# Token-tile stores and loads moved from SP's queue to ACT's, and eighteen expert-weight chunks allowed ahead of the gathers

## The chip, the cores and the metric

The kernel runs on one core of one Trainium2 chip. The metric is the device time of one execution in microseconds (us), and the number quoted for a kernel is the median of several executions.

## The reference

Two layers of a diffusion trunk work on 512 latent tokens and 256 context tokens of width 1024. Each layer normalises its rows, mixes the tokens in four head groups (HGRN2, Hyena, neighbourhood attention, latent attention), adds the result through one output projection, and then adds a mixture of 32 expert MLPs in which every token goes to its top two experts. Cut to the part around the change:

```
x  = x + g1 * (concat(o_a, o_b, o_c, o_d) @ w_out[l])           # residual rows
h2 = rmsnorm(x, norm2_g[l]) * (1 + s2) + sh2                    # normalised rows
lg = h2 @ wg + bg ; le = h2 @ we + be                           # router: 4 groups, 8 experts in each
wts = softmax(top_2(le of the best group)) * p(best group)
y   = sum over the 2 experts e of  wts * ((silu(h2 @ w_gate[e]) * (h2 @ w_up[e])) @ w_down[e])
x  = x + g2 * y                                                 # layer 0 does this for the context rows too
```

Layer 0 handles 768 tokens, which are six tiles of 128; layer 1 handles only the 512 latent tokens, four tiles.

## The kernel before, in words

After the mixers of a layer, the output projection is done in four column blocks `c` (the matmuls have line L1787). In the last block, each finished tile of 128 tokens is passed, two tiles later (`LAG = 2`), to `token_tile(t)`. That function stores the residual rows to DRAM (L1753, into `acc` in layer 0 and into the output in layer 1), transposes the rows on TensorE (L1757), takes the row's inverse root mean square (`row_rs`, whose square on ACT is L1170), copies the transposed rows out of PSUM on ACT (L1759), and multiplies them by the router's weights (L1762). Every fourth tile it also loads the norm gain (`E.load`, L170) and the two modulation rows (`bc_row`, L1511), and VectorE joins two of them (L1766). VectorE then scales the rows (L1768), GpSimd adds the shift (L1769), the normalised rows are stored to DRAM (L1770, `h2d`), and VectorE finishes the logits (L1772). The router (`rt.tile`, VectorE rows L891 to L936 with ACT rows L905 and L912) follows tile by tile, one tile behind, and `rt.finish()` builds the tables from which the gathers know which token goes where.

The MoE then works through the experts in blocks of 64 tokens. GpSimd gathers the normalised rows of a block (128 half rows of 2 KB) from `h2d` with an indirect DMA (L990), TensorE transposes them (L1000), multiplies by the gate and up weights (L1012) and by the down weights (L1039), and GpSimd scatters the weighted result into the residual (L1052).

The expert weights are 201 MB in each layer: 32 experts of six chunks of 1 MB. `Weights.fetch` issues one DMA for each chunk (L1378) on SP's queue into one of 18 slots, so three experts fit. A slot is loaded again when the matmuls that read it are done. Among the chunks that are fetched without an `after`, chunk q also waits until chunk q - 5 has landed (`FLIGHT = 5`). `EARLY` sets how many chunks are fetched before the token tiles (4 in layer 0, 7 in layer 1), and `FIRST` up to which chunk SP goes on without waiting for the first gather: 12 in layer 0 and 16 in layer 1. The rest of the first 18 chunks waits in `moe` for the first gather, by `wts.fetch(18, E.gathered)` at L1109. Ten of the slots lie in a buffer named `side`, which the mixers use before, and the others in `arena`.

Each engine's queue runs its instructions, DMA issues among them, in order: an issue that waits holds back everything behind it on that engine. A scheduler lays out the instructions of each engine ahead of time, so the program order of one engine can change wherever an instruction changes its engine. The completion of a DMA is signalled by one of a few semaphores, which all the queues fed by SP and ACT share; a DMA that takes up such a semaphore again waits until the DMA that used it before has landed.

Of the kernel before, what the change touches and what calls it, by code (L numbers as in the profile page):

```python
# [18 lines left out]
P = 128  # L19
NLAT, NCTX, NTOK = 512, 256, 768  # L20
DM = 1024
# [93 lines left out]
class Env:  # L115
# [48 lines left out]
    def p2(self):  # L164
        return self._ps("pa", 1024, 2)

    def load(self, tag, ap, bufs=1):

        t = self.t(tag, list(ap.shape[1:]), bufs=bufs, rows=ap.shape[0])
        self.nc.sync.dma_start(t, ap)  # L170
        return t

    def const(self, name, ap, dt=F32):
# [991 lines left out]
def row_rs(E, x, tag):  # L1165

    nc = E.nc
    rs = E.t(tag, 1, bufs=2)
    junk = E.t(tag + "j", DM, BF16, bufs=1)
    nc.scalar.activation(junk, x, AF.Square, accum_out=rs)  # L1170
    nc.vector.tensor_scalar(rs, rs, 1.0 / DM, EPS, op0=ALU.mult, op1=ALU.add)
    small_rsqrt(E, rs, tag)
    return rs
# [176 lines left out]
STEPS1 = [1] * 2  # L1350
STEPH1 = 13
HLM = 2
FIRST = (12, 16)
FLIGHT = 5
LAG = 2
AHEAD = 1
# [41 lines left out]
def half_rows(a, t):  # L1398

    return a[t * 256:(t + 1) * 256].rearrange("(p a) c -> p (a c)", a=2)  # L1400


def trunk(tc, d, out):
    nc = tc.nc
# [6 lines left out]
    with ExitStack() as top:  # L1411
# [3 lines left out]
        E = Env(tc, Arena(), None, cst)  # L1415
# [19 lines left out]
        h2d = [dr.tile([2 * (NTOK, NLAT)[l], 512], F32, name=f"h2d{l}") for l in range(2)]  # L1435
        acc = [dr.tile([2 * NTOK, 512], F32, name="acc"), out.rearrange("t (a c) -> (t a) c", a=2)]
# [65 lines left out]
        for l in range(2):  # L1502
# [2 lines left out]
            both = PARTS if full else PARTS[:1]  # L1505
            NQ = nt * P

            def bc_row(v, i, tag, bufs):
                r = E.t(tag, DM, bufs=bufs)
                a = modd[l][v:v + 1, i * DM:(i + 1) * DM]  # L1510
                nc.sync.dma_start(r, bass.AP(tensor=a.tensor, offset=a.offset, ap=[[0, P], [1, DM]]))  # L1511
                return r

            if l:
# [167 lines left out]
            def wo_half(c, h, load, cut):  # L1682

                if not h and load:
                    wos[c] = [wpools[c % 2][1].tile([P, 8, 256], F32R, tag=g, name=f"{g}{l}{c}", bufs=1) for g in ("woh", "wol")]
                hs = slice(h * 128, h * 128 + 128)
                if load:
                    raws[c, h] = wsc.t("wo", [8, 128], F32, 2, P)
                    nc.sync.dma_start(raws[c, h], d[f"w_out{l}"][c][:, :, hs])
                if cut:  # L1690
                    split_r(E, *(w[:, :, hs] for w in wos[c]), raws[c, h], 1)
# [25 lines left out]
            x1 = [E.t("x1", DM, bufs=nt) for _ in range(nt)]  # L1717
# [4 lines left out]
            br = E.load("br", d[f"b_rt{l}"])  # L1722
            n2c = E.load("n2c", d[f"n2c{l}"])
            g1 = [bc_row(v, 2, "g1", 2) for v in range(2 if full else 1)]


# [23 lines left out]

            def token_tile(t):
                v = t // 4
                nc.sync.dma_start(half_rows(acc[l], t), x1[t])  # L1753
                hTt = E.t("h2T", [8, P], bufs=1)
                pt = E.p2()
                for j in range(8):
                    nc.tensor.transpose(pt[:, j * P:(j + 1) * P], x1[t][:, j * P:(j + 1) * P], E.c["ident"])  # L1757
                rs = row_rs(E, x1[t], "rs2")
                nc.scalar.copy(hTt, pt.rearrange("p (j t) -> p j t", j=8))  # L1759
                ps = E.p1()  # L1760
                for j in range(8):
                    nc.tensor.matmul(ps[:, :36], hTt[:, j], wa[v][:, j], start=(j == 0), stop=(j == 7))  # L1762
                if t % 4 == 0:
                    n2 = E.load("h2", d[f"n2g{l}"], bufs=2)
                    mod[:] = [bc_row(v, 4, "rsc", 1), bc_row(v, 3, "rsh", 1)]
                    nc.vector.scalar_tensor_tensor(mod[0], mod[0], 1.0, n2, op0=ALU.add, op1=ALU.mult)  # L1766
                h2 = E.t("h2", DM, bufs=2)
                nc.vector.scalar_tensor_tensor(h2, x1[t], rs, mod[0], op0=ALU.mult, op1=ALU.mult)  # L1768
                nc.gpsimd.tensor_add(h2, h2, mod[1])  # L1769
                nc.sync.dma_start(half_rows(h2d[l], t), h2)  # L1770
                lg = E.t("rlg", 36, bufs=2)
                nc.vector.scalar_tensor_tensor(lg, ps[:, :36], rs, cb[v], op0=ALU.mult, op1=ALU.add)  # L1772
                return lg

            mod, logits = [], []
            for c in range(4):
                if c:
                    wo(c)
                woh, wol = wos[c]
                for t in range(nt + LAG * (c == 3)):  # L1780
                    if t < nt:
                        tt, cc = slice(t * P, (t + 1) * P), slice(c * 256, c * 256 + 256)
                        ps = E.pw()
                        i = 0
                        for o_, w in ((oh, woh), (oh, wol), (ol, woh)):
                            for k in range(8):
                                nc.tensor.matmul(ps[:, :256], o_[:, k, tt], w[:, k, :], start=(i == 0), stop=(i == 23))  # L1787
                                i += 1
                        tmp = E.t("xo", 256, bufs=2)
                        nc.vector.tensor_mul(tmp, ps[:, :256], g1[t // 4][:, cc])  # L1790
                        nc.gpsimd.tensor_add(x1[t][:, cc], x1[t][:, cc], tmp)  # L1791
                    if c == 3 and t >= LAG:
                        logits.append(token_tile(t - LAG))
                        if t > LAG:
                            rt.tile(t - LAG - 1, logits[t - LAG - 1])
# [9 lines left out]
            wts.grow(18 - len(wts.slots))  # L1805
            wts.fetch(FIRST[l])
            sps.close()
# [4 lines left out]
            for v in range(2 if full else 1):  # L1812
                g = E.t("g2", 512, bufs=2)
                a = modd[l][v:v + 1, 5 * DM:]
# [134 lines left out]
```

## Time and profile before

| what | value |
|---|---|
| median of 3 runs | 2420.07 us (2411.84 to 2425.87) |
| the profiled execution | 2419.79 us |
| its span, first to last instruction | 2418.0 us |
| mean granted TensorE clock | 0.956 of full speed |
| busy shares of the span | PE 84%, DVE 41%, ACT 24%, POOL 22% |

The profiled execution took 2419.79 us, 1.8 us more than its span and 0.3 us less than the median of the runs, so it stands for them well. Below, PE is TensorE's matmuls, DVE is VectorE, POOL is GpSimd, SP is the sync engine whose work here is to issue DMAs, and "SPq" is its queue. Times in the views count from the start of the span. In layer 0 the token tiles run from about 745 to 805 us and the MoE from 818 us to about 1320 us; in layer 1 the token tiles run from about 1865 to 1900 us and the MoE from 1916 us to the end.

### The profile page before, as it was taken

Reading aid. Unit: us, or ns where it says so; the run is one execution under the profiler, and the core shown is the slowest. Engines: PE = TensorE matmul, PEld = TensorE weight load, DVE = VectorE, ACT = ScalarE, POOL = GpSimd, SP = SyncE. Lnnn points to the kernel's source line nnn. Section 1 sums busy time; section 2 is a strip of 40 time slices with the busy share of each in tenths; the row PEclk is TensorE's granted clock in tenths of the full one; section 3 lists DMA queues with packets and bytes.
Section 4 is the critical chain, followed back from the end, with each engine's and each line's share of the span. In section 5 each row is a group of like instructions: output and inputs, shape, how many; then the busy total and the mean of one; then the engine's idle time right before and its main releaser. Section 6 shows DMA issues by size and latency. Waiting matters only on the chain. (4 is left out here: it accounts for less than half of the span.)

```text
span 2418.0 us, 32200 instructions
## 1 busy us (share of the span) xinstructions
PE 2039.0 (84%) x11540; PEld 1186.2 (49%) x11540; DVE 999.4 (41%) x2435; ACT 573.2 (24%) x1138; POOL 537.2 (22%) x429
## 2 busy tenths in 40 slices
PE   5789999999999598887777598999899598877775
PEld 1458778766688333322222386686669333222221
DVE  6751865537746522221112437645584511111110
ACT  4433431344622100000000234314352100000000
POOL 1653413211013122211111225131102221111111
PEclk9999999999998699999999799999999699999998
DMA  6434524202244899999999425420233899999996
GB/s 242 165 116 176 194 105 147 81 9 69 85 143 142 299 378 387 405 401 404 400 395 411 173 92 175 147 103 18 86 126 133 313 393 410 409 408 409 410 403 258
DMA packets 139311, 581.54 MB, mean 241 GB/s; under 512 B 23984, under 2 KB 47873, under 8 KB 88630
## 3 DMA queue, kind: packets, MB, share of 16 engines
q1 hardware_dynamic: 124054, 555.89, 59.5%
q0 software_dynamic: 15008, 22.36, 3.9%
q8 instruction: 152, 2.49, 0.4%
q14 instruction: 97, 0.79, 0.1%
HBM read 554.17 MB, written 36.80 MB: 244 GB/s over the span
## 5 line engine op out<-in xcount | busy, mean ns | idle before, releaser
L1012 PE MATMUL pb<-side,arena 128*64 128x512 f32 x1224 | 288.9, 604 | 45.9 <-DMA side<-in_w_moe 42.2
L1016 DVE COPY arena<-pb 128x512 f32<-128x512 f32 x67 | 46.3, 691 | 501.5 <-PE pb L1012 501.5
L1012 PE MATMUL pb<-arena 128*64 128x512 f32 x920 | 217.9, 605 | 41.8 <-DMA arena<-in_w_moe 38.2
L1028 ACT ACTIVATE arena<-pb 128x256 f32<-128x256 f32 x67 | 25.7, 383 | 902.9 <-PE pb L1025 902.9
L1276 POOL TENSOR_TENSOR wl<-side,wh 128x1024 fp32r<-128x1024 f32 x52 | 125.4, 2412 | 395.5 <-ACT wh L1275 267.1
L1012 PEld LDWEIGHTS pb<-side,arena 128*64 128x64 f32 x1224 | 81.4, 137 | 246.5 <-issue 126.4
L1300 PE MATMUL pw<-hh,wh 128*128 128x512 f32 (+1 forms) x720 | 168.6, 366 | 3.1 <-DVE arena L495 1.9
L1300 PE MATMUL pw<-hh,wl 128*128 128x512 f32 (+1 forms) x720 | 160.5, 358 | 0.0
L1043 DVE SCALAR_TENSOR_TENSOR arena<-pb,arena 128x512 f32<-128x512 f32 x67 | 50.3, 750 | 263.2 <-PE pb L1039 254.5
L1039 PE MATMUL pb<-side,arena 128*64 128x512 f32 x576 | 137.8, 617 | 24.9 <-DVE arena L1029 20.4
L1300 PE MATMUL pw<-hl,wh 128*128 128x512 f32 (+1 forms) x720 | 158.2, 355 | 0.0
L1012 PEld LDWEIGHTS pb<-arena 128*64 128x64 f32 x920 | 62.2, 138 | 190.8 <-issue 96.0
L1052 POOL DMA_INDIRECT acc<-arena x35 | 55.2, 1577 | 387.8 <-DVE arena L1047 338.5
L1300 PEld LDWEIGHTS pw<-hh,wh 128*128 128x128 f32 x720 | 117.8, 190 | 36.1 <-issue 14.4
L1039 PE MATMUL pb<-arena 128*64 128x512 f32 x496 | 115.5, 599 | 21.3 <-DVE arena L1029 20.8
L1300 PEld LDWEIGHTS pw<-hh,wl 128*128 128x128 f32 x720 | 117.9, 189 | 25.1 <-issue 9.9
L1300 PEld LDWEIGHTS pw<-hl,wh 128*128 128x128 f32 x720 | 117.4, 189 | 24.4 <-issue 8.7
L1052 POOL DMA_INDIRECT out_dram<-arena x32 | 50.9, 1590 | 311.4 <-DVE arena L1043 297.2
L990 POOL DMA_INDIRECT arena<-h2d,arena x67 | 69.8, 1042 | 187.5 <-issue 56.0
L1791 POOL TENSOR_TENSOR arena<-arena 128x256 f32<-128x256 f32 x40 | 31.2, 782 | 292.2 <-DVE arena L1790 278.2
L1025 PE MATMUL pb<-ident,arena 128*128 128x128 f32 x268 | 42.4, 280 | 55.4 <-DVE arena L1016 55.4
L1039 PEld LDWEIGHTS pb<-side,arena 128*64 128x64 f32 x576 | 39.0, 140 | 101.5 <-issue 60.8
(367 smaller groups left out, 3444.2 us busy)
## 6 DMA issues: line engine op xcount, KB each, us to landing
side<-in_w_moe SPq DMA_DIRECT2D x215, 1024.0 KB
arena<-in_w_moe SPq DMA_DIRECT2D x169, 1024.0 KB
arena<-in_w_ada SPq DMA_DIRECT2D x53, 512.0 KB
side<-in_w_in SPq DMA_DIRECT2D x52, 512.0 KB
side<-in_w_ada SPq DMA_DIRECT2D x43, 512.0 KB
arena<-in_w_out SPq DMA_DIRECT2D x16, 512.0 KB
arena<-in_x SPq DMA_DIRECT2D x12, 512.0 KB
spd<-arena SPq DMA_DIRECT2D x23, 256.0 KB
```

What stands on the lines that cost most here:

```text
L990: E.gathered = nc.gpsimd.indirect_dma_start(out=xg, out_offset=None, in_=h2d, in_offset=bass.IndirectOffsetOnAxis(ap=gi, axis=0), **(dict( ...
L1012: nc.tensor.matmul(pg[64 * s:64 * s + 64], xT[:, j // 4, j % 4, :], W[j // 2][:, (j % 2) * 1024 + s * 512:(j % 2) * 1024 + s * 512 + 512], ...
L1016: nc.vector.tensor_copy(gu, pg)
L1025: nc.tensor.transpose(pt[:, c * 128:(c + 1) * 128], gu[:, c * 128:(c + 1) * 128], E.c["ident"])
L1028: nc.scalar.activation(hT, pv[:, :, 0, :], AF.Silu)
L1039: nc.tensor.matmul(pd[64 * s:64 * s + 64], hT[:, c, :], W[4 + c // 2][:, (c % 2) * 1024 + s * 512:(c % 2) * 1024 + s * 512 + 512], start=( ...
L1043: nc.vector.scalar_tensor_tensor(y, pd, w[0], g2[0], op0=ALU.mult, op1=ALU.mult)
L1052: E.nc.gpsimd.indirect_dma_start(out=acc, out_offset=bass.IndirectOffsetOnAxis(ap=si, axis=0), in_=y, in_offset=None, compute_op=ALU.add, ...
L1276: (nc.vector if k % 2 else nc.gpsimd).tensor_sub(lo, src, hi.bitcast(F32))
L1300: nc.tensor.matmul(ps[:, :n], w[:, j, :], h[:, j, a:a + n], start=(i == 0), stop=(i == 23))
L1791: nc.gpsimd.tensor_add(x1[t][:, cc], x1[t][:, cc], tmp)
```

## The change

Three things are edited. The two stores of `token_tile` (L1753, L1770) are issued from ACT's queue instead of SP's. The loads of the norm gain and of the two modulation rows in `token_tile` go to ACT's queue as well, through a new argument `queue` of `load` and `bc_row`. That is 18 DMAs in layer 0 (6 + 6 stores, 2 gain loads, 4 modulation rows) and 11 in layer 1 (4 + 4, 1, 2). And `FIRST` becomes 18 in both layers, so chunks 12 to 17 of layer 0 and 16 and 17 of layer 1 no longer wait for the first gather.

```
-    def load(self, tag, ap, bufs=1):
+    def load(self, tag, ap, bufs=1, queue=None):
         t = self.t(tag, list(ap.shape[1:]), bufs=bufs, rows=ap.shape[0])
-        self.nc.sync.dma_start(t, ap)
+        (queue or self.nc.sync).dma_start(t, ap)
...
-FIRST = (12, 16)
+FIRST = (18, 18)
...
-            def bc_row(v, i, tag, bufs):
+            def bc_row(v, i, tag, bufs, queue=nc.sync):
                 r = E.t(tag, DM, bufs=bufs)
                 a = modd[l][v:v + 1, i * DM:(i + 1) * DM]
-                nc.sync.dma_start(r, bass.AP(tensor=a.tensor, offset=a.offset, ap=[[0, P], [1, DM]]))
+                queue.dma_start(r, bass.AP(tensor=a.tensor, offset=a.offset, ap=[[0, P], [1, DM]]))
...
             def token_tile(t):
-                nc.sync.dma_start(half_rows(acc[l], t), x1[t])
+                nc.scalar.dma_start(half_rows(acc[l], t), x1[t])
...
-                    n2 = E.load("h2", d[f"n2g{l}"], bufs=2)
-                    mod[:] = [bc_row(v, 4, "rsc", 1), bc_row(v, 3, "rsh", 1)]
+                    n2 = E.load("h2", d[f"n2g{l}"], bufs=2, queue=nc.scalar)
+                    mod[:] = [bc_row(v, 4, "rsc", 1, nc.scalar), bc_row(v, 3, "rsh", 1, nc.scalar)]
...
-                nc.sync.dma_start(half_rows(h2d[l], t), h2)
+                nc.scalar.dma_start(half_rows(h2d[l], t), h2)
```

What stands on SP's queue in layer 0 from the fourth token tile on, before (the expert chunks are L1378 and the rows L1815 load the output gate of the MoE):

```order
L170 DMA arena<-in_n2g 128x1024
L1378 DMA side_6263<-in_w_moe 128x2048
L1770 DMA h2d_70<-arena 128x1024
L1511 DMA arena<-modd_66 128x1024 x2
L1753 DMA acc<-arena 128x1024
L1378 DMA side_6263<-in_w_moe 128x2048
L1770 DMA h2d_70<-arena 128x1024
L1378 DMA side_6263<-in_w_moe 128x2048
L1770 DMA h2d_70<-arena 128x1024
L1378 DMA side_6263<-in_w_moe 128x2048 x5
L1815 DMA arena<-modd_66 128x1x512 x2
```

The first three chunks stand between stores and loads of the token tiles, and the other five behind the last store. SP's queue at the same place after the change, from the last loads of the output projection's weights (L1689) on:

```order
L1719 DMA arena<-in_x 128x1024 x3
L1689 DMA arena<-in_w_out 128x8x128 x4
L1378 DMA side_6263<-in_w_moe 128x2048 x10
L1378 DMA arena<-in_w_moe 128x2048 x4
L1815 DMA arena<-modd_66 128x1x512 x2
```

No store and no token-tile load is left between the chunks, and the four `arena` chunks (14 to 17) stand ahead of the gate loads and of the first gather.

ACT's queue in the middle of layer 0's token tiles, around the loads of the second set of gain and modulation rows (L905 and L912 are router rows):

```order
+L1770 DMA h2d_70<-arena 128x1024
 L905 ACTIVATE arena<-arena 128x4
-L1759 COPY arena<-pa_5849 128x1024
+L1759 COPY arena<-pa_6030 128x1024
+L170 DMA arena<-in_n2g 128x1024
+L912 ACTIVATE arena<-arena 128x1
+L1511 DMA arena<-modd_66 128x1024 x2
+L905 ACTIVATE arena<-arena 128x4
+L912 ACTIVATE arena<-arena 128x1
+L1753 DMA acc<-arena 128x1024
```

The loads of the second set now stand behind the copy L1759 of the fifth tile (`pa_6030`).

ACT's queue in the token tiles of layer 1, from the first tile's copy on:

```order
 L1759 COPY arena<-pa_19343 128x1024
+L1770 DMA h2d_71<-arena 128x1024
+L1753 DMA out_dram<-arena 128x1024
+L1770 DMA h2d_71<-arena 128x1024
+L1759 COPY arena<-pa_19408 128x1024
+L905 ACTIVATE arena<-arena 128x4
+L912 ACTIVATE arena<-arena 128x1
 L1170 ACTIVATE arena<-arena 128x1024
-L905 ACTIVATE arena<-arena 128x4
-L1759 COPY arena<-pa_19408 128x1024
-L912 ACTIVATE arena<-arena 128x1
+L1753 DMA out_dram<-arena 128x1024
```

The square L1170 of the third tile, which stood ahead of the second tile's copy, now stands behind two stores of normalised rows, that copy and two router rows. Layer 0 has the same pattern at its third tile.

## Rows read from the trace of the kernel before

**Rows 1.** Waits on SP's queue, 942:1320 (total us, times, longest):
```profile
SPq L1378 <- DMA side<-in_w_moe: 169.8, 71, 3.5
```

**Rows 2.** Windows: busy per engine, then PEclk, DMA share, GB/s:
```profile
770.00:830.00 60.00, 36.09 (x181) 25.09 (x179) 38.82 (x242) 9.82 (x24) 13.85 (x10) 0.60 0.81 277
905.00:930.00 25.00, 22.58 (x112) 8.20 (x110) 6.24 (x10) 1.94 (x4) 4.21 (x3) 1.00 0.94 355
1935.00:1940.00 5.00, 5.00 (x26) 1.65 (x24) 0.75 (x1) 0.00 (x0) 1.63 (x1) 1.00 0.80 292
2220.00:2240.00 20.00, 14.03 (x68) 4.85 (x68) 2.98 (x5) 1.94 (x4) 2.63 (x2) 1.00 1.02 410
```

**Rows 3.** SP's timeline, 1025 to 1085 us (start, length, count):
```profile
1032.65 19.74 SPq L1378 DMA_DIRECT2D arena<-in_w_moe  x8
1083.22 0.33 SPq L1378 DMA_DIRECT2D arena<-in_w_moe  x1
```

**Rows 4.** Waits on SP's queue, 770 to 835 us:
```profile
SPq L1770 <- POOL arena L1769: 22.4, 3, 14.4
```

**Rows 5.** SP's timeline, 745 to 830 us:
```profile
776.56 1.21 SPq L1511 DMA_DIRECT2D arena<-modd  x2
778.33 0.44 SPq L1378 DMA_DIRECT2D side<-in_w_moe  x1
793.62 0.42 SPq L1378 DMA_DIRECT2D side<-in_w_moe  x1
820.57 1.42 SPq L1378 DMA_DIRECT2D side<-in_w_moe  x2
```

**Rows 6.** Waits on SP's queue, 905 to 942 us:
```profile
SPq L1378 <- PE pb L1012: 12.7, 9, 4.3
SPq L1378 <- PE pb L1039: 10.4, 4, 5.4
```

**Rows 7.** SP's timeline, three stretches between 905 and 926 us:
```profile
905.29 0.33 SPq L1378 DMA_DIRECT2D side<-in_w_moe  x1
912.64 5.48 SPq L1378 DMA_DIRECT2D side<-in_w_moe  x4
925.00 0.33 SPq L1378 DMA_DIRECT2D side<-in_w_moe  x1
```

**Rows 8.** ACT's timeline, token tiles of layer 0, then layer 1:
```profile
782.76 1.01 ACT L1759 COPY arena<-pa 128x1024 f32<-128x1024 f32 x1 [0.23 <-PE pa L1757]
1874.60 1.06 ACT L1170 ACTIVATE arena<-arena 128x1024 bf16<-128x1024 f32 x1 [4.91 <-DVE arena L1772]
1879.83 0.29 ACT L912 ACTIVATE arena<-arena 128x1 f32<-128x1 f32 x1 [1.74 <-DVE arena L891]
```

**Rows 9.** VectorE's timeline, 786 to 792 us:
```profile
787.73 1.22 DVE L1766 SCALAR_TENSOR_TENSOR arena<-arena 128x1024 f32<-128x1024 f32 x1
791.10 2.13 DVE L892 SCALAR_TENSOR_TENSOR arena<-arena,miota 128x4 f32<-128x4 f32 x1
```

**Rows 10.** GpSimd's timeline, layer 0 and layer 1:
```profile
812.19 1.25 POOL L990 DMA_INDIRECT arena<-h2d,arena  x1 [13.30 <-DVE arena L948]
1874.34 2.35 POOL L1769 TENSOR_TENSOR arena<-arena 128x1024 f32<-128x1024 f32 x1 [2.11 <-DVE arena L1768]
1882.41 2.37 POOL L1769 TENSOR_TENSOR arena<-arena 128x1024 f32<-128x1024 f32 x1 [3.11 <-DVE arena L1768]
1911.46 1.07 POOL L990 DMA_INDIRECT arena<-h2d,arena  x1 [18.84 <-DVE arena L964]
```

**Rows 11.** TensorE's timeline, 817 to 820 us:
```profile
818.01 1.09 PE L1000 MATMUL pb<-ident,arena 128*128 128x128 f32 x4 [8.17 <-DMA arena<-h2d,arena]
```

**Rows 12.** Waits on SP's queue, 1876 to 1920 us:
```profile
SPq L1770 <- POOL arena L1769: 15.3, 3, 6.1
```

**Rows 13.** Waits and timeline of SP's queue, 1920 to 1955 us:
```profile
SPq L1378 <- PE pb L1012: 11.0, 6, 5.3
1935.50 0.82 SPq L1378 DMA_DIRECT2D arena<-in_w_moe  x2
```

## The prediction, made before the changed kernel ran

> **What bounds the kernel now.** I read the waits of SP's queue first, since the change is about that queue. In the long stretch of layer 0's MoE, 942 to 1320 us, SP stands in front of expert chunks until earlier chunks have landed: 169.8 us for the `side` slots alone [rows 1]. The reader should then look at the busy windows: in the MoE of layer 1 the DMA engines are full (share 1.02 at 410 GB/s) while TensorE is busy for 14.03 of 20 us [rows 2]. So the MoE is bound by moving weights, and the pace can be read off: 18 chunks lie between the issues at 1032.65 and 1083.22 (eight issues from the first row on, ten in `side` slots, then the second row) [rows 3], which is 50.57 / 18 = 2.81 us per chunk, 16.9 us per expert of six. A microsecond in which the engines stand idle before the end of that stream costs a microsecond, unless something else sets the stream's place.
>
> The token tiles are the place where they idle. From 770 to 830 us the DMA share is 0.81 [rows 2], so 60 x 0.19 = 11.4 us of the engines' time is free there, and SP stands 22.4 us in front of stores of normalised rows, waiting for GpSimd's addition [rows 4]. The chunk behind the issue at 778.33 goes out only at 793.62, 15.3 us later [rows 5]; and the last six of layer 0's first 18 chunks wait for the gather and go out from 820.57 [rows 5]. In layer 1 the same wait is 15.3 us [rows 12].
>
> But a lead gained here must survive the start of the MoE. There are only 18 slots, and a slot comes free when TensorE has read it. From 905 to 942 us SP waits 12.7 + 10.4 = 23.1 us for TensorE's matmuls [rows 6], and in layer 1 11.0 us between 1920 and 1955 [rows 13]. There the stream is placed by TensorE, which started when the gathers landed. Chunks that were fetched earlier only make SP reach full slots earlier.
>
> **Part 1: the lead, layer 0.** Six chunks may go out before the gather, worth 6 x 2.81 = 16.9 us if nothing else limited them. What can be kept is the work that the engines still have in hand at the last slot that TensorE gives late. At 905.29 a chunk is issued [rows 7] and, by the limit of five in flight, at most 5 x 2.81 = 14.1 us of chunks are outstanding, done at 919.4. Four more issues begin at 912.64 [rows 7], 11.2 us more, done at 930.6. The next, which TensorE sets, comes at 925.00 [rows 7]. So at that moment 5.6 us of chunks are in hand; with a longer lead they would have landed before, and the chunk of 925.00 would land up to 5.6 us sooner. Bounds: 5.6 and 0 (the share of 0.94 from 905 to 930 [rows 2] says that the engines idled for 1.5 us even so). I take 4, since the backlog was worked out with five in flight at 905.29, the most there can be.
>
> **Part 2: the lead, layer 1.** Two chunks, 5.6 us at most, and 0 at least. The four chunks that TensorE released before 1935.50 are nearly through by then: the share falls to 0.80 in 1935 to 1940 [rows 2], just where the next pair is issued [rows 13]. I take 2.
>
> **Part 3: ACT waits in order.** One issue takes SP 0.33 us [rows 7]; if it takes ACT as long, the 29 DMAs are 9.6 us in two layers. In the token tiles of layer 0 ACT was busy for 9.82 of 60 us [rows 2], and the issues lie in its idle time, so I cost the issuing at nothing; without that cover it would be the 9.6 us. What counts are the waits behind which ACT's other rows now stand.
>
> In layer 1, the square of the third tile began at 1874.60 [rows 8]. Now it stands behind the store of the second tile's normalised rows, which waits for the addition of 1874.34 + 2.35 = 1876.7 [rows 10], and behind a copy and two router rows, the last of which ended at 1879.83 + 0.29 = 1880.1 [rows 8]. It can start at 1880.1 at the earliest, 5.5 us later. Its result is wanted by VectorE's scaling, whose addition on GpSimd began at 1882.41 [rows 10], so some of the 5.5 us is covered. If the tiles slide, GpSimd's additions fall among more of VectorE's last router rows, and beside an addition a VectorE row of some 0.2 us took 2.13 us [rows 9]. Bounds for the gather of layer 1: 0 and 7 us (5.5 and most of one such row); I take 3.
>
> In layer 0 the same pattern stands at the third tile, and the second set of modulation rows adds to it. Their loads were issued at 776.56 [rows 5]; on ACT they stand behind the copy that ended at 782.76 + 1.01 = 783.8 [rows 8], so they go out at least 7.2 us later. VectorE's row that joins them ran at 787.73 without an idle gap ahead of it [rows 9], 11.2 us after the issue; VectorE runs in order, so the router's rows wait behind it when it is late. If the loads land as slowly as 11.2 us, and the chunks now share the engines with them, the row moves to 783.8 + 11.2 = 795.0, 7.3 us later. If they land in under 3.9 us, it does not move. VectorE has router rows pulled ahead of it in the new order that fill some of the gap. Bounds for the gather of layer 0: 0 and 8; I take 2.
>
> **Part 4: gathers beside chunks.** The first gather of layer 0 began at 812.19 and TensorE used it at 818.01 [rows 10, 11], 5.8 us. Until now no chunk was issued between; now chunks 14 to 17 may be. Four chunks in full would be 4 x 2.81 = 11.2 us, but the gather moves 128 half rows of 2 KB, a quarter of a chunk, and goes from GpSimd's own queue. If the engines take turns, it needs its own 2.81 / 4 = 0.7 us once more. Bounds 0 and 3, I take 1 in each layer.
>
> A rule speaks against the whole change. The Trainium skill, "DMA: Bandwidth & Descriptors", section "Issuing engines are not separate DMA queues", says that DMAs from different engines end on the same 16 DMA engines and interleave, and that a second issuing engine saves only the sequencer's time to issue. By that rule alone the change would be worth the 9.6 us of issuing, none of it on the path. The trace disagrees in one point: SP's 22.4 us is a wait in order for a semaphore, not issuing, and that wait does leave the chunks' queue.
>
> **Part 5: the attention.** The scheduler has also moved the first set of loads (L1511) into ACT's stream amid the softmax. Nothing waits for them there for a long time; I take 0, with 2 us either way.
>
> **The sum.** Layer 0: 2 + 1 - 4 = -1. Layer 1: 3 + 1 - 2 = +2. Together +1 on the profiled 2419.79, or on the median of 2420.07, which lies 0.3 us off: 2421. With every term at its good end: -5.6 - 5.6 - 2 = -13, 2407. At its bad end: 8 + 7 + 3 + 3 + 2 = +23, 2443.
>
> **The rivals.** *The lead counts in full.* If slots were not the limit, eight chunks of 2.81 us, 22.5 us, would be kept: 2397. For it: the engines' free 11.4 us before the gather. Against it: SP's 23.1 us and 11.0 us of waits for TensorE. Chance 0.16.
>
> *Slower: the first gather of both layers is late.* TensorE's start sets the place of the stream, so a late gather is paid in full while the lead is lost in the slots. With 8 + 7 from ACT's order and 3 + 3 from the sharing: 2441. It decides from about 6 us in each layer, which makes 12 us, half a per cent. For it: an ACT row 5.5 us late in layer 1 and loads 7.2 us late in layer 0. Against it: the addition at 1882.41 leaves the third tile some cover, and the loads have slack where they land in less than 11.2 us. Chance 0.19.
>
> *The change does not do what it says.* The queues of SP and ACT share the semaphores on which completions are counted, so chunks 5 to 13 still wait until certain of ACT's stores and loads have landed, and chunk 14 takes its slot from a tile that the router frees only at its end. Then the lead is one or two chunks, and it is lost as above: 2420. Chance 0.12.
>
> **How the numbers follow.** The forecast holds 0.53, with its own range 2411 to 2432. Half a per cent, 12 us, is about what a measurement of this kernel tells from no change. Faster by more than that: the first rival and a little of the forecast, 0.19. Slower: the second rival and the forecast's far end, 0.21. Within: 0.60. The range leaves out the first rival alone, and takes in the second: 2402 to 2442.
>
> **What would show it.** Right: no store left on SP's queue, chunks 4 to 13 issued one behind the other from 772 us, the first gathers 1 to 5 us later than 812.19 and 1911.46, longer waits of SP for TensorE in the first experts, and the same 2.81 us per chunk afterwards. Wrong to the fast side: the last late slot of layer 0 at 920 or sooner, or no wait for TensorE at all. Wrong to the slow side: gathers more than 6 us late, or TensorE's first matmul more than 6 us behind its gather.

## The result, and the profile after

The changed kernel took 2430.07 us in the median of 12 runs (2425.72 to 2440.34), the kernel before 2416.29 us in the median of 12 runs on the same chips. The ratio is 1.0064 with a 95% interval of 1.0051 to 1.0076, so the change costs 15 us, 12 to 18. The time lies inside the range of 2402 to 2442, but it is not the forecast of 2421: it is slower by a little over half a per cent, which had a chance of 0.21.

The profiled execution of the changed kernel has a span of 2425.8 us, 7.8 us more than before. That difference has to be taken apart, because a part of it lies where nothing was changed. I cut both spans at the same landmarks: the first matmul of the output projection (L1787), the issue of the first gather (L990), the first transpose of gathered rows (L1000), and the last up matmul of the layer (L1012). Here is TensorE's timeline of the kernel before at these landmarks (start, length):

```profile
684.40 1.19 PE L1787 MATMUL pw<-woh,oh 128*128 128x256 f32 x8
...
833.40 7.09 PE L1012 MATMUL pb<-arena 128*64 128x512 f32 x32 [2.04 <-ACT arena L1002]
...
1332.16 1.94 PE L1012 MATMUL pb<-side,arena 128*64 128x512 f32 x8 [0.67 <-DMA side<-in_w_moe]
...
1820.12 0.50 PE L1787 MATMUL pw<-woh,oh 128*128 128x256 f32 x2
...
1916.62 1.12 PE L1000 MATMUL pb<-ident,arena 128*128 128x128 f32 x4 [7.45 <-DMA arena<-h2d,arena]
...
2394.80 1.94 PE L1012 MATMUL pb<-side,arena 128*64 128x512 f32 x8 [0.96 <-SPq L1129]
```

The same of the changed kernel:

```profile
679.74 1.20 PE L1787 MATMUL pw<-woh,oh 128*128 128x256 f32 x8
...
821.76 1.09 PE L1000 MATMUL pb<-ident,arena 128*128 128x128 f32 x4 [10.00 <-DMA arena<-h2d,arena]
...
837.75 8.78 PE L1012 MATMUL pb<-arena 128*64 128x512 f32 x32 [2.67 <-ACT arena L1002]
...
1337.86 1.94 PE L1012 MATMUL pb<-side,arena 128*64 128x512 f32 x8 [0.57 <-DMA side<-in_w_moe]
...
1824.70 0.50 PE L1787 MATMUL pw<-woh,oh 128*128 128x256 f32 x2
...
1924.36 1.11 PE L1000 MATMUL pb<-ident,arena 128*128 128x128 f32 x4 [10.73 <-DMA arena<-h2d,arena]
...
2402.56 1.94 PE L1012 MATMUL pb<-side,arena 128*64 128x512 f32 x8 [0.28 <-SPq L1129]
```

GpSimd's timeline of the changed kernel, the first gather of each layer, which answers to [rows 10]:

```profile
814.12 1.25 POOL L990 DMA_INDIRECT arena<-h2d,arena  x1 [10.97 <-DVE arena L948]
...
1915.92 1.03 POOL L990 DMA_INDIRECT arena<-h2d,arena  x1 [11.37 <-DVE arena L964]
```

The differences of these rows give the stretches:

| stretch (us) | before | after | difference |
|---|---|---|---|
| layer 0: projection starts, to first gather issued | 127.79 | 134.38 | +6.6 |
| layer 0: first gather issued, to first transpose | 5.82 | 7.64 | +1.8 |
| layer 0: first transpose, to end of last up matmul | 516.09 | 518.04 | +2.0 |
| layer 1: projection starts, to first gather issued | 91.34 | 91.22 | -0.1 |
| layer 1: first gather issued, to first transpose | 5.16 | 8.44 | +3.3 |
| layer 1: first transpose, to end of last up matmul | 480.12 | 480.14 | 0.0 |

The six together are +13.6 us, which agrees with the medians. The rest of the span is 5.8 us shorter: layer 0's projection starts at 679.74 instead of 684.40, in front of which only the first set of modulation rows and the order of a few rows beside it have changed, and 1.1 us is gained between the MoE of layer 0 and the projection of layer 1. Over the ten kernels of this study that start lies anywhere between 678.2 and 687.5 us without a pattern, so it is the spread of single executions, and the stretches are what I compare below.

**Where the lead went.** SP's timeline of the changed kernel, layer 0:

```profile
764.83 29.65 SPq L1378 DMA_DIRECT2D side<-in_w_moe  x10
811.17 2.01 SPq L1378 DMA_DIRECT2D arena<-in_w_moe  x4
```

The queue did what the diff says: no store stands between the chunks, the ten `side` chunks leave between 764.83 and 794.5 us, and the next four at 811.17, ahead of the gather. The six chunks that waited until 820.57 [rows 5] are all early. SP is not free of ACT's DMAs, though. A chunk that takes up a semaphore again waits for the store or load that used it last, so these waits stand in front of the chunks from 740 to 830 us, 25.3 us together:

```profile
SPq L1378 <- DMA h2d<-arena: 14.1, 2, 11.3
SPq L1378 <- DMA arena<-modd: 5.8, 2, 3.6
SPq L1378 <- DMA arena<-in_n2g: 5.4, 1, 5.4
```

Now look at the busy windows of the changed kernel (columns as in [rows 2]), right after the gathers and around the place where the prediction put the last late slot:

```profile
825.00:840.00 15.00, 12.11 (x51) 4.40 (x49) 1.11 (x2) 2.73 (x4) 1.44 (x2) 0.84 0.26 86
900.00:950.00 50.00, 45.27 (x222) 16.52 (x220) 13.50 (x22) 3.88 (x8) 8.46 (x6) 1.00 0.91 341
```

and of the kernel before:

```profile
825.00:840.00 15.00, 12.75 (x66) 5.32 (x64) 1.11 (x2) 2.73 (x4) 1.01 (x1) 1.00 1.02 365
900.00:950.00 50.00, 44.59 (x218) 16.29 (x216) 12.66 (x20) 3.87 (x8) 9.48 (x7) 1.00 0.98 380
```

From 825 to 840 us the DMA engines are busy for 0.26 of the time, where they were full before: all 18 slots are taken and none is free. TensorE goes through the first expert's weights twice, since its tokens fill two blocks, and the second block reads the same `arena` slots from 837.75 us on (the rows at 833.40 and 837.75 above); SP's next chunk leaves at 840.28. That is 11 us of idle engines, and the second window adds (0.98 - 0.91) x 50 = 3.5 us. Most of the 16.9 us of the lead is given back there. SP's waits from 830 to 960 us show it from the other side, 70 us for TensorE where the same rows of before come to 23.8 us (13.4 and 10.4):

```profile
SPq L1378 <- PE pb L1012: 50.8, 21, 16.6
SPq L1378 <- PE pb L1039: 19.5, 8, 6.5
```

**Where the time was lost.** ACT's timeline of the changed kernel (ACTq are the issues on its queue):

```profile
755.64 1.01 ACT L1759 COPY arena<-pa 128x1024 f32<-128x1024 f32 x1 [7.47 <-POOL arena L1769]
774.34 0.33 ACTq L1770 DMA_DIRECT2D h2d<-arena  x1
776.38 0.30 ACT L905 ACTIVATE arena<-arena 128x4 f32<-128x4 f32 x1 [5.17 <-DVE arena L904]
778.75 0.81 ACTq L1511 DMA_DIRECT2D arena<-modd  x2
...
1882.66 1.01 ACT L1759 COPY arena<-pa 128x1024 f32<-128x1024 f32 x1 [7.39 <-POOL arena L1769]
```

and VectorE's:

```profile
791.03 1.22 DVE L1766 SCALAR_TENSOR_TENSOR arena<-arena 128x1024 f32<-128x1024 f32 x1 [4.79 <-DMA arena<-modd]
```

The second set of modulation rows left at 778.75, 99.0 us after the projection's start, where SP had issued it 92.2 us after it (776.56 [rows 5]). After the store at 774.34, ACT's next row is a router row (L905) that waits for VectorE until 776.38, with 5.17 us without work ahead of it; behind it come a copy, the gain load and one more router row, and only then the two rows. The rows then landed so late that VectorE waited 4.79 us for them ahead of L1766; before, it had no idle gap there [rows 9]. From the projection's start, L1766 moved from 103.3 to 111.3 us, and the first gather behind it by 6.6.

The trace also holds the moment at which each DMA completes. Before, the first of the two rows landed at 783.10, 6.5 us after its issue, and so 4.6 us before L1766 ran. In the changed kernel it landed 12.3 us after its issue, and L1766 began at once. The 8.0 us of L1766 are therefore 6.8 us of later issue and 5.7 us of slower landing, less the 4.6 us that were to spare. Issued as late but landing as fast as before, the rows would have cost 2.2 us.

### The profile page after: what moved, and what is told of

It is laid out like the page before. It is cut to its first block, busy times and chain, and to the rows that moved or that the text cites. A ratio compares the mean times of both kernels' runs of the same rounds, so it can differ in the third digit from the quotient of the medians.

```text
span 2425.8 us, 32195 instructions
## 1 busy us (share of the span) xinstructions
PE 2034.7 (84%) x11540; PEld 1181.3 (49%) x11540; DVE 997.4 (41%) x2435; ACT 573.5 (24%) x1138; POOL 534.6 (22%) x429
## 5 line engine op out<-in xcount | busy, mean ns | idle before, releaser
L1012 PE MATMUL pb<-side,arena 128*64 128x512 f32 x1224 | 287.9, 605 | 42.8 <-DMA side<-in_w_moe 41.1
L1012 PE MATMUL pb<-arena 128*64 128x512 f32 x920 | 220.4, 610 | 40.3 <-DMA arena<-in_w_moe 36.2
L1012 PEld LDWEIGHTS pb<-side,arena 128*64 128x64 f32 x1224 | 82.1, 137 | 241.1 <-issue 128.8
L1043 DVE SCALAR_TENSOR_TENSOR arena<-pb,arena 128x512 f32<-128x512 f32 x67 | 50.3, 751 | 266.7 <-PE pb L1039 256.8
L1012 PEld LDWEIGHTS pb<-arena 128*64 128x64 f32 x920 | 62.6, 139 | 192.1 <-issue 101.1
L1039 PE MATMUL pb<-arena 128*64 128x512 f32 x496 | 118.7, 617 | 21.0 <-DVE arena L1029 20.2
L990 POOL DMA_INDIRECT arena<-h2d,arena x67 | 70.0, 1045 | 179.9 <-issue 63.3
```

The source lines that it names most:

```text
L990: E.gathered = nc.gpsimd.indirect_dma_start(out=xg, out_offset=None, in_=h2d, in_offset=bass.IndirectOffsetOnAxis(ap=gi, axis=0), **(dict( ...
L1012: nc.tensor.matmul(pg[64 * s:64 * s + 64], xT[:, j // 4, j % 4, :], W[j // 2][:, (j % 2) * 1024 + s * 512:(j % 2) * 1024 + s * 512 + 512], ...
L1039: nc.tensor.matmul(pd[64 * s:64 * s + 64], hT[:, c, :], W[4 + c // 2][:, (c % 2) * 1024 + s * 512:(c % 2) * 1024 + s * 512 + 512], start=( ...
L1043: nc.vector.scalar_tensor_tensor(y, pd, w[0], g2[0], op0=ALU.mult, op1=ALU.mult)
```

## The experiments

Two groups of runs were made. Each time is given as a ratio to the kernel before on the same chip, with the 95% interval. The table at the end of the section has the same six stretches for all.

**FIRST alone.** Everything stays on SP's queue:

```
-FIRST = (12, 16)
+FIRST = (18, 18)
```

> All stores and loads stay on SP's queue and only FIRST becomes (18, 18), so chunks 12 to 17 of layer 0 and 16 and 17 of layer 1 may go out ahead of the gathers. Theory A (the loss is made of the second set of modulation rows landing late and of gathers that land among the last chunks, while the lead is worth nothing because TensorE holds the slots): the modulation rows land as before and VectorE does not wait for them, but the gathers land later, by about 2 us in layer 0 and 3 us in layer 1: 4 to 7 us above before. Theory B (the loss comes from ACT's rows standing in order behind GpSimd's additions): ACT holds no store here, so within 3 us of before. Theory C (a lead pays where SP is not held up by stores): 5 us or more below before.

Measured: 1.0030 (1.0016 to 1.0043), 7 us slower. VectorE's L1766 has no idle gap, as before, and the path to the first gather is 1.5 us shorter in layer 0; but in layer 1 TensorE's first transpose comes 8.36 us after the gather's issue:

```profile
1918.49 1.11 PE L1000 MATMUL pb<-ident,arena 128*128 128x128 f32 x4 [10.66 <-DMA arena<-h2d,arena]
```

So more chunks ahead of the gathers cost time by themselves, at the gathers, and bring none. Theory B, for which nothing should have been lost, does not explain this part; theory C is out for the step from 12 to 18.

**The queue alone.** The stores and loads go to ACT's queue, and FIRST is left:

```
-FIRST = (18, 18)
+FIRST = (12, 16)
```

> All stores and token-tile loads on ACT's queue, FIRST stays (12, 16). Theory A: VectorE waits some 5 us for the second set of modulation rows in layer 0, because eight chunks now run ahead of and beside them; the first gathers of both layers land as fast after their issue as before (5 to 6 us): 4 to 8 us above before. Theory B: the whole loss stays, 12 us or more above before. Theory C: at or below before.

Measured: 1.0013 (1.0003 to 1.0024), 3 us slower, a little under what theory A gave. VectorE waits for the modulation rows, and the first gather of layer 0 is issued 6.8 us later after the projection's start, as in the changed kernel. But it lands 3.72 us after its issue: the chunks left earlier, on a free queue, and were through by then, which gives 2.1 us back. VectorE's timeline of this run at L1766:

```profile
797.41 1.23 DVE L1766 SCALAR_TENSOR_TENSOR arena<-arena 128x1024 f32<-128x1024 f32 x1 [3.93 <-DMA arena<-modd]
```

and TensorE's at the first transpose:

```profile
824.24 1.09 PE L1000 MATMUL pb<-ident,arena 128*128 128x128 f32 x4 [6.08 <-DMA arena<-h2d,arena]
```

**The loads back on SP.** The stores stay on ACT:

```
-                    n2 = E.load("h2", d[f"n2g{l}"], bufs=2, queue=nc.scalar)
-                    mod[:] = [bc_row(v, 4, "rsc", 1, nc.scalar), bc_row(v, 3, "rsh", 1, nc.scalar)]
+                    n2 = E.load("h2", d[f"n2g{l}"], bufs=2)
+                    mod[:] = [bc_row(v, 4, "rsc", 1), bc_row(v, 3, "rsh", 1)]
```

> The changed kernel, but the loads of the gain and the modulation rows are back on SP's queue, where the second set stands behind two chunks instead of five; the stores stay on ACT. Theory A: VectorE's wait for the modulation rows in layer 0 (4.8 us in the changed kernel) goes down to under 2 us and 4 to 6 us come back, while the gathers stay late: 5 to 9 us above before. Theory B: the waits of ACT's copies for GpSimd (7.5 us in each layer) are untouched, so it stays within 2 us of the changed kernel.

Measured: 1.0014 (1.0002 to 1.0027), 3 us slower; theory A had said 5 to 9. The rows leave 95.4 us after the projection's start, and VectorE's wait is down to 0.89 us. SP's timeline of this run at the rows:

```profile
777.24 1.06 SPq L1511 DMA_DIRECT2D arena<-modd  x2
```

VectorE's at L1766:

```profile
783.84 1.23 DVE L1766 SCALAR_TENSOR_TENSOR arena<-arena 128x1024 f32<-128x1024 f32 x1 [0.89 <-DMA arena<-modd]
```

The path to the first gather of layer 0 is 126.50 us, 1.3 us shorter than before, with all twelve stores of that layer on ACT. This is the strongest run against theory B: the stores on ACT are not what costs in layer 0. In layer 1 its profiled execution is 3.9 us longer on the same path, but there the output projection itself began at a granted clock of 0.50 (1.2 GHz), where before it was 1.00. The window of this run:

```profile
1820.00:1830.00 10.00, 10.00 (x53) 9.41 (x52) 1.38 (x6) 0.27 (x1) 0.00 (x0) 0.50 0.99 341
```

Behind the projection's last matmul, 1877.85 us, its gather comes after 36.9 us; before, it came 38.0 us after 1873.48.

**Only the chunks beside the gathers taken back.**

```
-FIRST = (18, 18)
+FIRST = (14, 15)
```

> The changed kernel with FIRST = (14, 15): the chunks that stand beside the gathers (14 to 17 and 15 to 17) wait for the first gather again, everything else as in the change. Theory A: the first gathers land 5 to 6 us after their issue as before instead of 7.6 and 8.4, so 4 to 7 us come back: 5 to 9 us above before. Theory B: within 2 us of the changed kernel, about 13 us above before.

Measured: 1.0030 (1.0019 to 1.0041), 7 us slower, in the range of theory A and half of the changed kernel's loss. The first gather of layer 0 lands after 3.74 us. In layer 1 it did not go as expected: 8.72 us. TensorE's first transposes of this run:

```profile
818.95 1.09 PE L1000 MATMUL pb<-ident,arena 128*128 128x128 f32 x4 [6.11 <-DMA arena<-h2d,arena]
...
1918.66 1.12 PE L1000 MATMUL pb<-ident,arena 128*128 128x128 f32 x4 [11.02 <-DMA arena<-h2d,arena]
```

The chunks that "wait for the first gather" in fact wait for the gather of the second expert (L1109 stands behind it). In layer 1 GpSimd issues that gather ahead of the first expert's, in every kernel here. So the chunks left at 1913.60, 3.7 us after the first issue of all, and ran beside the gather of the first expert, issued at 1912.86, for which TensorE waited until 1918.66. GpSimd also issued that gather 2.92 us behind the first one, where before it was 1.38 us; this is 1.5 of the 3.6 us by which the stretch is longer.

**The rows first, then the chunks.** In layer 0, chunk 6 is made to wait until the second set of rows has landed; the rest is the changed kernel:

```
-                queue.dma_start(r, bass.AP(...))
+                E.rows = queue.dma_start(r, bass.AP(...))
...
+            if full:
+                wts.fetch(6)
+                wts.fetch(7, E.rows)
             wts.fetch(FIRST[l])
```

> The changed kernel with one wait added: in layer 0 the third chunk after the output projection (number 6) waits until the second set of modulation rows has landed, so that two chunks instead of five run beside those loads; the program order of ACT is that of the changed kernel. Theory A: VectorE's wait for the rows (4.8 us in the changed kernel) is gone or under 1 us, the first gather of layer 0 is issued 4 to 5 us sooner after the start of the output projection, and the time is 3 to 6 us below the changed kernel (8 to 11 us above before). Theory B (ACT's in-order waits for GpSimd): no change from the changed kernel, 12 us or more above before. Theory C (a lead pays): slower than the changed kernel, since eight chunks leave 15 us later.

Measured: 1.0061 (1.0038 to 1.0085). The expected 3 to 6 us did not come back, but the run did not do what was expected of it either. The scheduler put chunks 7, 8 and 9 ahead of the waiting chunk 6 (the semaphores for which the later chunks wait show the order), so that five chunks, not two, left before the rows had landed, and the sixth behind them. SP's timeline of this run:

```profile
769.11 2.01 SPq L1378 DMA_DIRECT2D side<-in_w_moe  x4
...
781.23 0.33 SPq L1378 DMA_DIRECT2D side<-in_w_moe  x1
...
792.35 0.33 SPq L1378 DMA_DIRECT2D side<-in_w_moe  x1
```

VectorE's wait fell, but only from 4.79 to 1.98 us, by its timeline:

```profile
791.09 1.23 DVE L1766 SCALAR_TENSOR_TENSOR arena<-arena 128x1024 f32<-128x1024 f32 x1 [1.98 <-DMA arena<-modd]
```

L1766 ran 108.8 us after the projection's start, 2.5 us sooner than in the changed kernel and still 5.5 us later than before. The rows were issued at 781.62 and landed 9.4 us later; two chunks were moving beside them until 785.5 and 789.2. So this run does not tell how fast the rows would land on ACT's queue with the chunks out of the way.

The other runs tell a part of it. With the loads on ACT, two or three chunks were in flight when the rows were issued, and the first row landed after 12.3 us (the change), 11.4 (queue alone), 10.3 ((14, 15)) and 9.4 us (here). With the loads on SP, at most one was, and it landed after 3.3 to 6.7 us; in the run with the loads on SP four chunks left within 3.3 us behind the rows, and it still took 6.5 us. Whether the chunks ahead or the other queue makes the difference is not separated.

**A shorter lead.** The kernel before with four chunks fewer ahead of the gathers in layer 0:

```
-FIRST = (12, 16)
+FIRST = (8, 16)
```

> The kernel before with FIRST = (8, 16): four chunks of layer 0 that went out from 799.3 us, beside the first gather, wait for the gathers. Theory A (what counts is when the first gather lands; the lead is worth nothing as long as TensorE does not run out of chunks): the first gather of layer 0 lands some 3.7 us after its issue instead of 5.8 us, TensorE's first experts do not wait for a chunk, and the time is 1 to 3 us below before. Theory C (a lead pays): four chunks of 2.81 us less, 11 us above before.

Measured: 1.0036 (1.0020 to 1.0051), 9 us slower. Theory A fell here. The gather did land sooner, 3.76 us after its issue, but the MoE of layer 0 became 10.4 us longer: nearly the 4 x 2.81 = 11.2 us that theory C gave. SP's waits from 830 to 960 us show the other side of it:

```profile
SPq L1378 <- DMA side<-in_w_moe: 57.6, 22, 9.7
SPq L1378 <- PE pb L1012: 1.7, 6, 0.3
SPq L1378 <- PE pb L1039: 0.8, 3, 0.3
```

It hardly waits for TensorE any more, 2.5 us in all. The engines are behind from the start: from 800 to 815 us their share is 0.28, where in the kernel before it is 1.00. Each chunk that left later ends the stream later.

**No lead.** The kernel before again:

```
-FIRST = (12, 16)
+FIRST = (4, 7)
```

> The kernel before with FIRST = (4, 7): no chunk at all goes out between the early ones and the gathers, so the lead of layer 0 is eight chunks shorter and that of layer 1 nine. Theory A: in layer 0 the slots are still what TensorE gives, chunk 46, which goes out at 925 us, would land at about 818 + 43 x 2.81 = 939 us instead of 933, and 2 us come back from the gather: 3 to 5 us lost; in layer 1, where the slots hold SP only to about 1955 us, the stream would be at chunk 27 at 1915 + 21 x 2.81 = 1974 us instead of 1955: some 15 to 20 us lost. Together 17 to 25 us above before. Theory C with the full price of a lead: 17 x 2.81 = 48 us above before.

Measured: 1.0153 (1.0130 to 1.0176), 37 us slower. The MoE is 20.2 us longer in layer 0 for eight chunks, where theory A had 3 to 5, and 18.0 us longer in layer 1 for nine, as theory A worked out. So the whole lay between the theories.

**A version meant to beat both.** The run with the loads on SP, and FIRST between the two:

```
-FIRST = (18, 18)
+FIRST = (14, 16)
```

> A version meant to beat both: stores on ACT's queue, gain and modulation rows on SP's, FIRST = (14, 16), so that in layer 0 all chunks that go out early have landed before the first gather and the others wait for it. Theory A: modulation rows without a wait over 1 us, the first gather of layer 0 landing 3.7 us after its issue, router path 1 us shorter than before in both layers: 2 to 6 us below before. Theory B: ACT's waits stay, so 8 us or more above before.

Measured: 1.0001 (0.9988 to 1.0014), no difference from before. Its first transposes start 5.26 and 5.07 us after the gathers' issue, by TensorE's timeline of this run:

```profile
811.54 1.09 PE L1000 MATMUL pb<-ident,arena 128*128 128x128 f32 x4 [7.62 <-DMA arena<-h2d,arena]
...
1906.72 1.11 PE L1000 MATMUL pb<-ident,arena 128*128 128x128 f32 x4 [7.37 <-DMA arena<-h2d,arena]
```

The path of layer 1 is 1.8 us shorter, the MoE not at all. Three expectations failed: VectorE still waited 2.35 us for the modulation rows, the path of layer 0 was not shorter, and its gather took 5.26 us instead of 3.7, since the last of the early chunks landed at 807.1, behind the gather's issue at 806.28. The loss of the change is gone, and no gain was measured in its place.

All runs by the six stretches, as differences to before (path: projection's start to first gather; gather: its issue to the first transpose; MoE: from there to the last up matmul), their sum, and the measured ratio turned into us with 2416 us:

| kernel | path 0 | gather 0 | MoE 0 | path 1 | gather 1 | MoE 1 | sum | measured |
|---|---|---|---|---|---|---|---|---|
| the change | +6.6 | +1.8 | +2.0 | -0.1 | +3.3 | 0.0 | +13.6 | +15 (12 to 18) |
| FIRST alone | -1.5 | +1.4 | +1.9 | -0.6 | +3.2 | +1.1 | +5.5 | +7 (4 to 10) |
| queue alone | +6.8 | -2.1 | +1.6 | -0.8 | -0.1 | +0.6 | +6.0 | +3 (1 to 6) |
| loads on SP | -1.3 | +1.4 | +1.9 | +3.9 | +2.9 | -0.1 | +8.7 | +3 (0 to 7) |
| (14, 15) | +4.4 | -2.1 | -0.9 | +1.6 | +3.6 | +0.6 | +7.2 | +7 (5 to 10) |
| rows first | +4.1 | +1.9 | +1.7 | +0.8 | +3.2 | +0.4 | +12.1 | +15 (9 to 21) |
| (8, 16) | +1.8 | -2.1 | +10.4 | +0.5 | -0.1 | -1.1 | +9.4 | +9 (5 to 12) |
| (4, 7) | -1.4 | -2.1 | +20.2 | +0.2 | +1.8 | +18.0 | +36.7 | +37 (31 to 43) |
| loads on SP, (14, 16) | +0.3 | -0.6 | +0.7 | -1.8 | -0.1 | +0.3 | -1.2 | 0 (-3 to +3) |

The sums of single executions meet the measured times within about 3 us, but for the run with the loads on SP, whose low clock in layer 1 is named above. That is what makes the stretches usable.

## Why the prediction was right and wrong

**The number.** The sum said +1 us and +15 were measured. That the time lies inside the stated range is owed to the range's width, which was drawn to take in the slower rival.

**What bounds the kernel** was read rightly for the later part of each layer only. The prediction took the MoE as a stream of weights from the first gather on. But TensorE waits for no expert chunk until 1058.84 us in layer 0, 240.8 us behind the first transpose, and until 2082.01 us in layer 1, 165.4 us behind it. The first such wait of layer 0 in TensorE's timeline, of the kernel before, the changed kernel and the (8, 16) run:

```profile
1058.84 1.51 PE L1012 MATMUL pb<-arena 128*64 128x512 f32 x6 [1.17 <-DMA arena<-in_w_moe]
...
1065.02 1.94 PE L1012 MATMUL pb<-arena 128*64 128x512 f32 x8 [1.16 <-DMA arena<-in_w_moe]
...
999.49 1.94 PE L1012 MATMUL pb<-side,arena 128*64 128x512 f32 x8 [0.48 <-DMA side<-in_w_moe]
```

Up to there TensorE's own work sets the pace, and behind it the weights do. From the first gathered rows on the MoE takes 515 to 518 us in layer 0 and 479 to 481 us in layer 1 in every kernel with at least 12 and 15 chunks fetched early.

**Part 1 and Part 2, the lead,** were mis-sized, and Part 1 is the largest miss: gains of 4 and 2 us were taken, and the MoE became 2.0 us longer in layer 0 and stayed as it was in layer 1. The mechanism, slots held by TensorE, was right, and so, nearly, was the backlog at 925.00: by its completion, the chunk issued there landed 8.2 us after its issue, and in the changed kernel the same chunk landed 5.7 us after its own. The step that failed is to count that backlog as time of the layer. TensorE waited for no chunk there, so the sooner landing was of no use to it. What made the layer longer is TensorE's own work: the first expert's second block of up matmuls began 0.6 us later behind the first transpose and took 8.78 us instead of 7.09 (the rows at 837.75 and 833.40). The block behind it began 2.3 us later, and the first wait for a chunk came 243.3 us behind the first transpose instead of 240.8.

The runs with a shorter lead complete the picture. With four chunks ahead TensorE first waits for a chunk 50.3 us behind the first transpose, with eight 187.1 us behind it (the row at 999.49). The lead is worth 10.4 / 4 = 2.6 us per chunk from 8 to 12 chunks in layer 0, nearly its full price, and no gain was measured from 12 to 18: the kernel before stands near the point where more lead stops paying. That SP waits 23.8 us for TensorE there means the lead is about enough, not that time is lost.

**Part 3, layer 0,** is the second miss: 2 us taken, with bounds of 0 and 8, and 6.6 measured. The mechanism was named, loads issued at least 7.2 us later and VectorE standing in order in front of L1766. Against the projection's start they were issued 6.8 us later. The step that failed is the landing, for which 11.2 us was the slowest that I allowed. The rows really landed in 6.5 us before, and in 12.3 us beside the chunks of the changed kernel. That the chunks share the engines with the loads stood in the prediction, but without a price, and it is the larger part of that loss (5.7 us, against 2.2 for the later issue). The part that I counted as cover, router rows pulled ahead of L1766, was used up: VectorE still waited 4.79 us.

**Part 3, layer 1,** was taken at 3 and came out at -0.1. The third tile's square did start later, 6.4 us against the projection's start, behind a copy that waited 7.39 us for GpSimd's addition (the row at 1882.66 above). Its cover, the work that VectorE and the router had left, was complete. Behind the projection's last matmul the gather even came 1.1 us sooner, after 36.9 us instead of 38.0; every run with the stores on ACT shows 36.4 to 36.9 there, and every run with them on SP 38.0. The projection itself took 1.0 us longer; its first 10 us had a granted clock of 0.83, where before it was 1.00. The wait of one engine in order is no loss where no other engine runs out of work, and the same wait of 7.47 us in layer 0 cost nothing either, as the run with the loads on SP shows.

**Part 4** was taken at 1 us in each layer, and measured 1.8 and 3.3; the upper bound of 3 was a little too low for layer 1. The gather there shares the engines with three chunks issued just ahead of it. The Trainium skill, "DMA: Bandwidth & Descriptors", section "Queues, rings and completion order", says that each DMA engine takes turns between the queues it has work for, packet by packet. By turns of equal size, an estimate from that rule, the gather's own 0.7 us (256 KB at 2.81 us for 1 MB) would have been paid once more. The rows agree with the direction, and differ in the size: 5.16 us became 8.44. By the completions, the gather for which TensorE waits there landed 7.1 us after its issue instead of 3.7.

**The rule against the change** is that DMAs from any engine end on the same 16 DMA engines (the Trainium skill, same page, "Issuing engines are not separate DMA queues"). The rows agree with it: the free queue moved the chunks to the front, and the loads and gathers beside them landed later. They do not agree with its sentence that a second issuing engine saves the issue time only: in the queue-alone run the chunks were out of the gather's way, 2.1 us.

**Part 5** was 0 within 2 us. No wait for these loads stands ahead of the projection in the changed kernel, whose start moves by more than 2 us from execution to execution. Inside the projection VectorE waited 3.87 us for the first set's gain at 695.41, but the projection's matmuls took 85.0 us from first to last, before 88.1.

**The rivals.** The slower one had the right sign and the right two mechanisms, but asked for about 6 us or more in each layer; it was 10.4 in layer 0 (8.4 from path and gather, the rest from the MoE) and 3.2 in layer 1. The lead in full is excluded. That the change does not do what it says is excluded as well, though two of its details held: chunks did wait until ACT's stores and loads had landed, 25.3 us, and chunk 14 did wait for the router's last tile, to 811.17.

**What stays open.** The 2.0 us by which the MoE of layer 0 is longer with 18 chunks lie at the second block of the first expert, as said under Part 1. The granted clock fell there, to 1.2 GHz, by the busy window of the changed kernel:

```profile
839.00:842.40 3.40, 3.40 (x10) 1.19 (x8) 0.00 (x0) 0.00 (x0) 0.00 (x0) 0.50 0.34 75
```

TensorE had been idle for 10.00 us until 821.76, busy with the first block, and idle for 2.67 us until 837.75. The block took 8.78 or 8.79 us in five kernels (the change, FIRST alone, loads on SP, rows first, and loads on SP with (14, 16)) and 7.09 in the other five. What makes the clock fall in some of them was not tested; the idle time ahead of the block does not divide them, since it is 2.04 us in the kernel before and in the run with (14, 16). Open too is whether the modulation rows landed late because of the chunks ahead of them or because of their queue.

## What to carry to other kernels

Before giving a prefetch more lead, look at when the engine that uses it first waits for it. Here that wait moved from 187 to 241 us into the layer's MoE as the lead grew from 8 to 12 chunks, and no further with 18, apart from TensorE's own delay. The issuing queue tells it sooner: with eight chunks SP waited 57.6 us for earlier transfers to land and 2.5 us for TensorE, and four more chunks were worth 10.4 us; with twelve it waited 23.8 us for TensorE, and six more were worth nothing. When DMAs move to another engine's queue, follow the small loads first, not the stores: a load that another engine waits for in order now stands behind whatever its new queue waits for, and runs beside the large transfers that the old queue had held back. Compare single executions between landmarks on both sides of the change, since the untouched rest of this kernel moves by several us.

## What was not expected of the hardware

In layer 0 a gather of 256 KB was used 3.7 us after its issue where the chunks were through (queue alone, (14, 15), (8, 16) and (4, 7)), and 7.3 to 7.7 us after it with chunks of 1 MB issued just ahead. It goes with how far ahead the last of them left. Where it left 10.6 us before the gather (the kernel before, at 801.63) it took 5.8 us, 14.3 us before it (loads on SP with (14, 16)) 5.3 us, and 18.9 us before it ((14, 15)) 3.7 us.
